# Latent stage of a two-layer decoder trunk: the query norm's root, its factors and the value projections in another order

## The chip, the cores and the metric

One core of a Trainium2 chip runs the whole trunk in one launch. The metric is the device time of a run in microseconds (us); the median over the runs of a kernel is compared. TensorE does the matmuls, VectorE (DVE) and ScalarE (ACT) the element-wise work, GpSimd (POOL) a few small operations, SyncE (SP) issues the loads.

## The reference, cut to what matters

Two layers over 256 tokens of width 1024. Each layer is: half a SwiGLU feed-forward, a mixer beside an attention to 256 memory tokens, half a SwiGLU feed-forward. Layer 0 mixes with a short convolution; layer 1 with causal latent attention (MLA), 6 heads, whose keys and values come from one shared latent made after layer 0. The change lies in layer 1's mixer:

```
c_q, q_mem = split(h @ w_in, [384])
q = (rms_norm(c_q, g_q_lora) @ w_uq).reshape(b, s, 6, 192)
q_nope = rms_norm(q[..., :128], g_q_nope)
q_rope = apply_rope(rms_norm(q[..., 128:], g_q_rope), cos, sin)
v = (c_kv @ w_ukv).reshape(b, s, 6, 256)[..., 128:]
scores = (q_nope . k_nope + q_rope . k_rope) * 192 ** -0.5      # causal
y_mix = softmax(scores) @ v
y_mem = softmax(rms_norm(q_mem) . k_mem / 8) @ v_mem            # 4 heads of 64
x = x + concat(y_mix, y_mem) @ w_out
```

## The kernel before, in words

Everything is float32. Each weight unit (up to 128 x 1024) is loaded by SP into one of 6 raw buffers (L78) and split into a rounded high part (an ACT cast, L69) and the rest (a DVE subtraction, L70) in one of 8 split buffers. A product is then three matmuls (L203 to L205: high x high, high x low, low x high), in the feed-forward two (L209, L210). The class Stream keeps the units in one list in the order in which they are used: `get` takes the next one, `pump` issues loads up to 9 units and splits up to 5 units ahead of what has been taken. A pump inside `issue_after(ins)` holds those of its instructions that lie on the engine of `ins` behind `ins`.

The code is written in the Tile framework. The order in which the code emits operations is their priority; the framework orders each engine's instructions itself, and an operation that it holds to be ready may go ahead of an earlier one that is not. It also makes all the waits, and accesses of different engines to one PSUM bank are kept apart in time. PSUM has 8 banks: two called pg (`bank()`), two called pm (`mbank()`), four accumulators (`abank(q)`).

The function `mla` does layer 1's mixer:
- It projects the normalized input to the latent query (three blocks of 128) and the memory query (two blocks). The norm of the latent query isn't applied to it: the projections run on the raw latent, and its factor F (L1018) enters the later norms through F and its square F2 (L1020).
- For each half t of the tokens it projects the rotary part of the query (`uq`), multiplies by the gain (L998), sums squares (L1003, L1004) and rotates: half 0 on DVE, half 1 on POOL (`apply_rope`, L814 to L820, six operations; both use the same temporary buffers).
- `next(mem)` runs the first part of the memory attention: column sums of the squared memory query (L615), the variance (L623, L177), the root as a power on POOL (L162, tile rsy_mq), the factor mq_rs (L632). The generator `mem_attention` gives control back at each `yield`.
- The latent query's sum of squares (L1011), variance, root on POOL (L162, tile rsy_cq), F and F2.
- Three pairs of heads are projected (the query projections, L203 to L205 with out acc or pg); each pair is copied by DVE (L1048), then squared by ACT (L1050).
- Column sums of the squares (L1058, 24 matmuls with one column each) give the heads' variances (L1063 to L1066), a root in DVE steps (L165 to L172) and the factors ra and rs (L1070 to L1074).
- Scores without the rotary part for heads 0 to 3 (L1028, in the four accumulators); the memory attention's first scores, maxima and exponentials (L641 to L658).
- `next(kv_steps)` twice: the value projections, the last steps of the generator `shared_kv` (its function `project` with s = 1; 4 times 6 matmuls of 384 columns on the latent in tiles mem_V and mem_kT), each copied out of its bank by ACT (L939).
- The rotated queries are scaled by ra (L1082) and transposed (L1086, L1087), and a pump is held behind the scaling. Scores of heads 4 and 5, rotary scores (L1093), and then softmax, transposes and value products head by head (`soft` L1100 to L1115, `value` L1121 to L1129), mixed with the steps of the memory attention (L667 to L678) by a written list, and with the output projection, which begins as soon as an accumulator is free.

Of the kernel before, what the change touches and what calls it, by code (L numbers as in the profile page):

```python
# [16 lines left out]
P = 128  # L17
# [91 lines left out]
def trunk(ctx: ExitStack, tc: tile.TileContext, a, out):  # L109
# [498 lines left out]

    def mem_attention(l, q, sq, F, outs, pe_tile):

        cs = mbank()
        for b in range(2):
            for t in range(2):
                o = 4 * t + 2 * b
                nc.tensor.matmul(cs[:, 0, o:o + 2], sq[:, b, t * P:(t + 1) * P], half2, start=(b == 0 and t == 0),  # L615
                                 stop=(b == 1 and t == 1), skip_group_check=True)
        csv = cs[:, 0, 0:8].rearrange("p (t h) -> p t h", t=2)
        if F is not None:
            fb = F.rearrange("p (t o) -> p t o", o=1).broadcast_to([P, 2, 4])
            f2 = sm.tile([P, 2], F32, name="mq_f2")  # L620
            nc.vector.tensor_tensor(out=f2, in0=F, in1=F, op=ALU.mult)
            v0 = sm.tile([P, 2, 4], F32, name="mq_v0")
            nc.vector.tensor_tensor(out=v0, in0=csv, in1=f2.rearrange("p (t o) -> p t o", o=1).broadcast_to([P, 2, 4]),  # L623
                                    op=ALU.mult)
            csv = v0
        v = mean_eps(csv, 64, [P, 2, 4], "mq")
        y = rsqrt(v, [P, 2, 4], "mq")
        rs = sm.tile([P, 2, 4], F32, name="mq_rs")
        if F is None:
            nc.vector.tensor_scalar(out=rs, in0=y, scalar1=0.125, scalar2=None, op0=ALU.mult)  # L630
        else:
            nc.vector.scalar_tensor_tensor(out=rs, in0=y, scalar=0.125, in1=fb, op0=ALU.mult, op1=ALU.mult)  # L632
        kT, mv = mem_st[l]
        yield
        for b in range(2):
            pes = []
            scs = [mbank(), mbank()]
            for t in range(2):
                for hh in range(2):
                    rows = slice(64 * hh, 64 * hh + 64)  # L640
                    nc.tensor.matmul(scs[hh][:, t, :], q[rows, b, t * P:(t + 1) * P], kT[rows, b, :], start=(t == 0),  # L641
                                     stop=(t == 1), skip_group_check=True)
            for hh in range(2):
                h = 2 * b + hh
                sc = scs[hh]
                mx = sm.tile([P, 2], F32, name="m_mx")
                nc.vector.tensor_reduce(out=mx, in_=sc, axis=AX.X, op=ALU.max)
                nb = sm.tile([P, 2], F32, name="m_nb")
                nc.vector.scalar_tensor_tensor(out=nb, in0=mx, scalar=-1.0, in1=rs[:, :, h], op0=ALU.mult, op1=ALU.mult)
                pe = pe_tile()  # L650
                se = sm.tile([P, 2], F32, name="m_se")
                for t in range(2):
                    nc.scalar.activation(out=pe[:, t, :], in_=sc[:, t, :], func=AF.Exp, bias=nb[:, t:t + 1],
                                         scale=rs[:, t, h:h + 1], accum_out=se[:, t:t + 1])
                rc = sm.tile([P, 2], F32, name="m_rc")
                nc.vector.reciprocal(out=rc, in_=se)
                for t in range(2):
                    nc.vector.tensor_scalar(out=pe[:, t, :], in0=pe[:, t, :], scalar1=rc[:, t:t + 1], scalar2=None,  # L658
                                            op0=ALU.mult)
                pes.append(pe)  # L660
            yield
            pts = []
            for hh in range(2):
                tp = mbank()
                for mt in range(2):
                    for t in range(2):
                        nc.tensor.transpose(tp[:, mt, t * P:(t + 1) * P], pes[hh][:, t, mt * P:(mt + 1) * P], ident)  # L667
                pt = wk.tile([P, 2, T], F32, name="sq")
                nc.scalar.copy(out=pt, in_=tp)
                pts.append(pt)  # L670
            yield
            g = keep(6 + b)
            ob = mbank()
            for mt in range(2):
                for hh in range(2):
                    h = 2 * b + hh
                    rows = slice(64 * hh, 64 * hh + 64)
                    nc.tensor.matmul(ob[rows, 0, :], mv[:, mt, 64 * h:64 * h + 64], pts[hh][:, mt, :], start=(mt == 0),  # L678
                                     stop=(mt == 1), skip_group_check=True)
            split(ob[:, 0, :], None, g[:, 0, :], g[:, 1, :])  # L680
            outs[6 + b] = g
            if b == 0:
                yield
            else:
                nc.scalar.activation(out=warm, in_=pe[:, 0, 0:1], func=AF.Silu, scale=0.0)
# [138 lines left out]
    def shared_kv():  # L824
# [70 lines left out]
        yield  # L895

        def project(s, c, t, w):
            b = (bank() if s else mbank()).rearrange("p a t -> p (a t)")[:, 0:384]
            for kt in range(2):
                mm3(b, (ct[kt][:, 0, t * P:(t + 1) * P], ct[kt][:, 1, t * P:(t + 1) * P]),  # L900
                    (w[:, 0, kt * 384:(kt + 1) * 384], w[:, 1, kt * 384:(kt + 1) * 384]), kt == 0, kt == 1)
            return b
# [44 lines left out]
    def mla(next_norm, pl, kv_steps):  # L947
# [43 lines left out]
        for t in range(2):  # L991
            b = abank(t).rearrange("p a t -> p (a t)")[:, 0:384]
            for k in range(3):
                ww, o = (wu0, k * 384) if k < 2 else (wu1, 0)
                mm3(b, (cq[k][:, 0, t * P:(t + 1) * P], cq[k][:, 1, t * P:(t + 1) * P]),
                    (ww[:, 0, o:o + 384], ww[:, 1, o:o + 384]), k == 0, k == 2)
            q1 = big1[:, 768 + 384 * t:1152 + 384 * t].rearrange("p (h d) -> p h d", d=64)
            nc.vector.tensor_tensor(out=q1, in0=b.rearrange("p (h d) -> p h d", d=64),  # L998
                                    in1=gc[:, GC_GQR:GC_GQR + 64].rearrange("p (o d) -> p o d", o=1).broadcast_to([P, 6, 64]),
                                    op=ALU.mult)  # L1000
            sq = wk.tile([P, 2, T], F32, name="sq")
            sqv = sq.rearrange("p a t -> p (a t)")[:, 0:384]
            nc.scalar.activation(out=sqv, in_=b, func=AF.Square)  # L1003
            nc.vector.tensor_reduce(out=msr[:, t, :], in_=sqv.rearrange("p (h d) -> p h d", d=64), axis=AX.X, op=ALU.add)  # L1004
            q2 = keep(14, (P, 6, 64), F32) if t else big1[:, 1536:1920].rearrange("p (h d) -> p h d", d=64)
            apply_rope(nc.gpsimd if t else nc.vector, q1, q2, t, 6, m_tile)
            rps.append(q2)
        next(mem)
        cs = mbank()
# [4 lines left out]
        nc.vector.tensor_tensor(out=rq2, in0=rq, in1=rq, op=ALU.mult)  # L1014
        v = sm.tile([P, 2], F32, name="cq_v")
        nc.vector.tensor_tensor(out=v, in0=cs[:, 0, 0:2], in1=rq2, op=ALU.mult)
        F = sm.tile([P, 2], F32, name="cq_F")
        nc.vector.tensor_tensor(out=F, in0=rsqrt(mean_eps(v, 384, [P, 2], "cq"), [P, 2], "cq"), in1=rq, op=ALU.mult)  # L1018
        F2 = sm.tile([P, 2], F32, name="cq_F2")
        nc.vector.tensor_tensor(out=F2, in0=F, in1=F, op=ALU.mult)  # L1020
        krT, knT, V = kv["krT"], kv["knT"], kv["V"]
        def out_of(sc, t):
            return (sc[:, 0:P], sc[:, P:384])[t]
# [5 lines left out]
                                 stop=False, skip_group_check=True)  # L1029
            return sc  # L1030

        cs = bank()
        sqs = []
        for pr in range(3):
            b = abank(2 + pr) if pr < 2 else bank()
            for s in range(2):
                n = 2 * pr + s
                if n == 0:
                    w, o = wu1, 384
                elif n % 2 == 1:  # L1040
                    w, o = W.get(("uq", 2 + n // 2)), 0
                else:
                    o = 384
                for k in range(3):
                    oo = o + k * P
                    mm3(b[:, s, :], (w[:, 0, oo:oo + P], w[:, 1, oo:oo + P]), (cq[k][:, 0, :], cq[k][:, 1, :]),
                        s == 0 and k == 0, s == 1 and k == 2)
            nc.vector.tensor_copy(out=qn[:, 2 * pr:2 * pr + 2, :], in_=b)  # L1048
            sq = (wk.tile([P, 2, T], F32, name="sq") if pr < 2 else ev.tile([P, 2, T], F32, name="ev"))
            nc.scalar.activation(out=sq, in_=b, func=AF.Square)  # L1050
            sqs.append(sq)
            if pr == 0:
                W.pump()
        for pr, sq in enumerate(sqs):
            for s in range(2):
                for t in range(2):
# [17 lines left out]
        nc.vector.scalar_tensor_tensor(out=rs, in0=y[:, 0], scalar=192.0 ** -0.5, in1=Fb, op0=ALU.mult, op1=ALU.mult)  # L1074
        scs = [scores(h) for h in range(4)]
        next(mem)
        next(kv_steps)
        next(kv_steps, None)
        for t in range(2):
            q2 = rps[t]  # L1080
            q3 = big1[:, 768 + 384 * t:1152 + 384 * t].rearrange("p (h d) -> p h d", d=64)
# [246 lines left out]
```

## Time and profile before

| what | value |
|---|---|
| median of 3 runs | 970.01 us (969.94 to 973.65) |
| the profiled execution | 971.22 us |
| its span, first to last instruction | 969.4 us |
| mean granted TensorE clock | 0.996 |
| TensorE busy | 958.2 us, 99% of the span |
| VectorE busy | 718.0 us, 74% |
| ScalarE busy | 558.7 us, 58% |
| GpSimd busy | 40.3 us, 4% |

All other times come from one execution that the hardware profiler recorded; they count from the start of its span. A busy TensorE is not TensorE at its peak: matmuls are pipelined, and their ends are modelled. The granted clock is the share of full speed (2.4 GHz) that TensorE had; the lower of its two levels is 1.2 GHz. The latent stage lies between about 704 and 785 us, where the last feed-forward begins.

### The profile page before, as it was taken

Reading aid. Unit: us, or ns where it says so; the run is one execution under the profiler, and the core shown is the slowest. Engines: PE = TensorE matmul, PEld = TensorE weight load, DVE = VectorE, ACT = ScalarE, POOL = GpSimd, SP = SyncE. Lnnn points to the kernel's source line nnn. Section 1 sums busy time; section 2 is a strip of 40 time slices with the busy share of each in tenths; the row PEclk is TensorE's granted clock in tenths of the full one; section 3 lists DMA queues with packets and bytes.
Section 4 is the critical chain, followed back from the end, with each engine's and each line's share of the span. In section 5 each row is a group of like instructions: output and inputs, shape, how many; then the busy total and the mean of one; then the engine's idle time right before and its main releaser. Section 6 shows DMA issues by size and latency. Waiting matters only on the chain.

```text
span 969.4 us, 15411 instructions
## 1 busy us (share of the span) xinstructions
PE 958.2 (99%) x5856; PEld 848.8 (88%) x5856; DVE 718.0 (74%) x1225; ACT 558.7 (58%) x963; POOL 40.3 (4%) x62
## 2 busy tenths in 40 slices
PE   9999999999999999999999999999999999999998
PEld 7889898889898888888888888888997988888887
DVE  7988767774978787777839877778558679777771
ACT  8766555554556465555645666556455666555550
POOL 1300000000000000000000300000020000000000
PEclk9999999999999999999999999999998999999999
DMA  8786556552744485555526755654523318666530
GB/s 310 238 278 204 197 192 190 180 195 67 256 157 130 142 272 196 195 174 196 194 64 205 255 196 175 200 191 161 175 96 130 111 53 290 204 195 196 179 128 17
DMA packets 50187, 174.10 MB, mean 180 GB/s; under 512 B 5696, under 2 KB 7232, under 8 KB 50112
## 3 DMA queue, kind: packets, MB, share of 16 engines
q1 hardware_dynamic: 49680, 172.45, 53.9%
q8 instruction: 46, 0.75, 0.3%
q10 hardware_dynamic: 432, 0.66, 0.2%
q14 instruction: 29, 0.24, 0.1%
HBM read 172.04 MB, written 1.05 MB: 179 GB/s over the span
## 4 chain that ended last, share of the span: by engine, by line
PE 88%; DVE 7%; DMA 2%; POOL 1%; ACT 1%; issue 1%; SPq 0%; DVEq 0%
PE pg L209 20%; PE pm L209 19%; PE pg L210 10%; PE pm L210 10%; PE acc L209 9%; PE acc L210 4%; DVE whl L70 3%; PE pg L203 2%; PE pg L204 2%; PE pg L205 2%; PE pm L203 2%; PE pm L205 2%; PE pm L204 2%; DMA wraw<-in_w 1%; PE acc L203 1%; PE acc L204 1%
## 5 line engine op out<-in xcount | busy, mean ns | idle before, releaser
L70 DVE TENSOR_TENSOR whl<-wraw,whl 128x1024 fp32r<-128x1024 f32 (+3 forms) x330 | 390.2, 1198 | 92.6 <-ACT whl L69 92.4
L69 ACT CAST whl<-wraw 128x1024 fp32r<-128x1024 f32 (+3 forms) x330 | 337.5, 1029 | 163.4 <-PE pm L210 80.6
L209 PE MATMUL pg<-xs,whl 128*128 128x512 f32 x704 | 255.7, 397 | 1.0 <-DVE ev L492 0.9
L209 PE MATMUL pm<-xs,whl 128*128 128x512 f32 x704 | 254.9, 396 | 0.5 <-DVE ev L492 0.5
L210 PE MATMUL pg<-xs,whl 128*128 128x256 f32 x704 | 196.8, 280 | 0.2 <-DVE whl L70 0.2
L210 PE MATMUL pm<-xs,whl 128*128 128x256 f32 x704 | 196.1, 279 | 0.0
L209 PEld LDWEIGHTS pm<-xs,whl 128*128 128x128 f32 x704 | 132.2, 188 | 31.5 <-DVE ev L492 0.8
L209 PEld LDWEIGHTS pg<-xs,whl 128*128 128x128 f32 x704 | 132.2, 188 | 31.4 <-DVE ev L492 1.0
L209 PE MATMUL acc<-g,whl 128*128 128x512 f32 x384 | 138.7, 397 | 0.9 <-DVE g L196 0.9
L210 PEld LDWEIGHTS pg<-xs,whl 128*128 128x128 f32 x704 | 132.6, 188 | 2.1 <-DVE whl L70 1.8
L210 PEld LDWEIGHTS pm<-xs,whl 128*128 128x128 f32 x704 | 132.5, 188 | 0.3
L210 PE MATMUL acc<-g,whl 128*128 128x256 f32 x384 | 107.0, 279 | 0.0
L209 PEld LDWEIGHTS acc<-g,whl 128*128 128x128 f32 x384 | 72.0, 188 | 19.0 <-DVE g L196 2.4
L210 PEld LDWEIGHTS acc<-g,whl 128*128 128x128 f32 x384 | 72.3, 188 | 0.0
L491 ACT COPY sq<-pm 128x256 f32<-128x256 f32 x88 | 32.8, 372 | 68.5 <-PE pm L210 68.5
L209 PE MATMUL pg<-g,whl 128*128 128x512 f32 x192 | 68.3, 398 | 0.0
L195 ACT CAST g<-gg 128x256 fp32r<-128x256 f32 x94 | 38.0, 405 | 49.7 <-DVE gg L508 45.3
L496 DVE TENSOR_TENSOR ev<-ev,R 128x512 f32<-128x512 f32 x88 | 61.1, 698 | 2.3
L209 PE MATMUL pm<-g,whl 128*128 128x512 f32 x170 | 60.4, 398 | 0.0
L492 DVE TENSOR_TENSOR ev<-pm,sq 128x256 f32<-128x256 f32 x88 | 37.2, 423 | 27.5 <-ACT sq L491 27.3
L203 PE MATMUL pg<-xs,whl 128*128 128x256 f32 x192 | 55.3, 288 | 0.0
L505 ACT ACTIVATE silu<-ev 128x256 f32<-128x256 f32 x88 | 36.5, 415 | 31.5 <-DVE ev L496 28.8
(323 smaller groups left out, 1352.5 us busy)
## 6 DMA issues: line engine op xcount, KB each, us to landing
wraw<-in_w SPq DMA_DIRECT2D x260, 512.0 KB, 4.1
wraw<-in_cin SPq DMA_DIRECT2D x20, 512.0 KB, 4.1
wraw<-in_wo SPq DMA_DIRECT2D x16, 512.0 KB, 4.3
wraw<-in_wmem SPq DMA_DIRECT2D x8, 512.0 KB, 4.3
wraw<-in_qin SPq DMA_DIRECT2D x5, 512.0 KB, 4.5
wraw<-in_mem SPq DMA_DIRECT2D x4, 512.0 KB, 3.8
wraw<-in_wukv SPq DMA_DIRECT2D x4, 384.0 KB, 3.3
wraw<-in_uq SPq DMA_DIRECT2D x4, 384.0 KB, 3.5
```

Source lines behind the costliest of these rows:

```text
L69: nc.scalar.copy(out=h[:, 0, o:o + n], in_=r[:, o:o + n])
L70: nc.vector.tensor_tensor(out=h[:, 1, o:o + n], in0=r[:, o:o + n], in1=h[:, 0, o:o + n].bitcast(F32), op=ALU.subtract)
L195: first = nc.scalar.copy(out=hi, in_=src)
L203: nc.tensor.matmul(o, lhs[0], rhs[0], start=start, stop=False, skip_group_check=True)
L204: nc.tensor.matmul(o, lhs[0], rhs[1], start=False, stop=False, skip_group_check=True)
L205: nc.tensor.matmul(o, lhs[1], rhs[0], start=False, stop=stop, skip_group_check=True)
L209: nc.tensor.matmul(o, lhs[0], x, start=start, stop=False, skip_group_check=True)
L210: nc.tensor.matmul(o[:, 0, :], lhs[1], x[:, 0, :], start=False, stop=stop, skip_group_check=True)
L491: nc.scalar.copy(out=part[:, s, :], in_=ps[s][:, 1, :])
L492: nc.vector.tensor_tensor(out=e[:, s, :], in0=ps[s][:, 0, :], in1=part[:, s, :], op=ALU.add)
L496: evac = nc.vector.tensor_tensor(out=e, in0=e, in1=rb(st["R"]), op=ALU.mult)
L505: act = nc.scalar.activation(out=sl, in_=e[:, 0, :], func=AF.Silu)
```

## The change

Four edits, all in the functions printed above. In `mem_attention`, control goes back right behind the root, so that mq_rs is emitted with the memory scores. In `shared_kv`, the value projections of the second token half take a pm bank instead of a pg bank. In `mla`, the rotation of half 1 on POOL is emitted behind the latent query's root, and F and F2 are made later. The two steps of the value projections, and the bank of the column sums, are emitted right behind the query projections.

```
@@ mem_attention
         y = rsqrt(v, [P, 2, 4], "mq")
+        yield
         rs = sm.tile([P, 2, 4], F32, name="mq_rs")
...
         kT, mv = mem_st[l]
-        yield
@@ shared_kv
         def project(s, c, t, w):
-            b = (bank() if s else mbank()).rearrange("p a t -> p (a t)")[:, 0:384]
+            b = (bank() if s and not t else mbank()).rearrange("p a t -> p (a t)")[:, 0:384]
@@ mla
-            apply_rope(nc.gpsimd if t else nc.vector, q1, q2, t, 6, m_tile)
+            if t == 0:
+                apply_rope(nc.vector, q1, q2, t, 6, m_tile)
             rps.append(q2)
         next(mem)
...
-        F = sm.tile([P, 2], F32, name="cq_F")
-        nc.vector.tensor_tensor(out=F, in0=rsqrt(mean_eps(v, 384, [P, 2], "cq"), [P, 2], "cq"), in1=rq, op=ALU.mult)
-        F2 = sm.tile([P, 2], F32, name="cq_F2")
-        nc.vector.tensor_tensor(out=F2, in0=F, in1=F, op=ALU.mult)
+        y_cq = rsqrt(mean_eps(v, 384, [P, 2], "cq"), [P, 2], "cq")
+        apply_rope(nc.gpsimd, q1, rps[1], 1, 6, m_tile)
...
-        cs = bank()
         sqs = []
         for pr in range(3):
...
+        next(kv_steps)
+        next(kv_steps, None)
+        cs = bank()
+        F = sm.tile([P, 2], F32, name="cq_F")
+        nc.vector.tensor_tensor(out=F, in0=y_cq, in1=rq, op=ALU.mult)
+        F2 = sm.tile([P, 2], F32, name="cq_F2")
+        nc.vector.tensor_tensor(out=F2, in0=F, in1=F, op=ALU.mult)
         for pr, sq in enumerate(sqs):
...
         scs = [scores(h) for h in range(4)]
         next(mem)
-        next(kv_steps)
-        next(kv_steps, None)
         for t in range(2):
```

## Rows read from the trace of the kernel before

**Rows 1.** The page: busy time, share of the span and instructions of each engine.

```profile
PE 958.2 (99%) x5856; PEld 848.8 (88%) x5856; DVE 718.0 (74%) x1225; ACT 558.7 (58%) x963; POOL 40.3 (4%) x62
```

**Rows 2.** Stretches: us, busy of PE, PEld, DVE, ACT, POOL, PE clock, DMA share, GB/s.

```profile
721.00:726.00 5.00, 3.03 (x26) 2.89 (x25) 1.77 (x6) 2.40 (x4) 1.43 (x3) 1.00 0.00 0
726.00:733.20 7.20, 7.20 (x30) 5.44 (x28) 3.22 (x13) 0.57 (x2) 0.00 (x0) 0.53 0.25 75
733.20:749.00 15.80, 14.17 (x89) 11.21 (x89) 15.22 (x42) 11.41 (x32) 0.00 (x0) 1.00 0.49 166
749.00:785.00 36.00, 36.00 (x278) 33.91 (x274) 26.06 (x66) 27.63 (x68) 0.00 (x0) 1.00 0.28 89
```

**Rows 3.** The chain that ended last, 716 to 724: start, us, what.

```profile
716.65 0.59 POOL g L814
...
717.79 1.59 POOL rsy_mq L162
...
721.85 0.68 POOL rsy_cq L162
...
722.90 0.60 DVE xs L1048
...
723.60 0.61 ACT sq L1050
```

**Rows 4.** Timeline of PE, 721 to 749: start, us, what [idle before <- releaser].

```profile
721.33 0.95 PE L1058 MATMUL pg<-ones,sq 128*128 128x1 f32 x8
724.25 1.05 PE L1058 MATMUL pg<-ones,sq 128*128 128x1 f32 x8 [1.97 <-ACT sq L1050]
725.16 3.01 PE L1028 MATMUL acc<-spare,xs 128*128 128x128 f32 x12
...
733.43 0.34 PE L204 MATMUL pg<-whl,mem_V 128*128 128x384 f32 x1
...
736.23 0.34 PE L205 MATMUL pg<-whl,mem_kT 128*128 128x384 f32 x1
737.62 0.44 PE L203 MATMUL pg<-whl,mem_V 128*128 128x384 f32 x1 [1.05 <-ACT spare L939]
...
739.90 0.92 PE L1028 MATMUL pg<-spare,xs 128*128 128x128 f32 x4
740.66 0.71 PE L667 MATMUL pm<-ident,g 128*128 128x128 f32 x5
...
748.01 0.61 PE L1121 MATMUL pm<-ident,g 128*128 128x128 f32 x3 [0.58 <-DVE g L1115]
```

**Rows 5.** Timeline of DVE, 709 to 744.

```profile
709.34 0.96 DVE L70 TENSOR_TENSOR whl<-wraw,whl 128x768 fp32r<-128x768 f32 x1 [0.24 <-ACT whl L69]
...
726.10 1.23 DVE L70 TENSOR_TENSOR whl<-wraw,whl 128x1024 fp32r<-128x1024 f32 x1 [1.72 <-ACT whl L69]
729.70 0.17 DVE L1063 TENSOR_TENSOR vv<-pg,cq_F 128x12 f32<-128x12 f32 x1 [2.37 <-PE pg L1058]
...
731.85 0.18 DVE L170 SCALAR_TENSOR_TENSOR rst_qh<-rsy_qh 128x24 f32<-128x24 f32 x1
733.19 0.69 DVE L647 TENSOR_REDUCE m_mx<-pm 128x2 f32<-128x512 f32 x1 [1.16 <-PE pm L641]
...
735.13 0.56 DVE L1082 TENSOR_TENSOR xs<-xs,q_ra 128x384 f32<-128x384 f32 x1
...
739.52 3.49 DVE L70 TENSOR_TENSOR whl<-wraw,whl 128x1024 fp32r<-128x1024 f32 x3
743.30 1.02 DVE L1100 TENSOR_TENSOR ev<-acc,mask 128x384 f32<-128x384 f32 x2 [0.29 <-PE acc L1093]
```

**Rows 6.** Timeline of ACT, 724 to 738.

```profile
724.09 1.98 ACT L69 CAST whl<-wraw 128x1024 fp32r<-128x1024 f32 x2
...
737.07 0.88 ACT L939 COPY spare<-pg 128x384 f32<-128x384 f32 x2
```

**Rows 7.** The chain that ended last, layer 0's memory scores, at full clock.

```profile
271.67 1.06 PE pm L641 x8
```

## The prediction

> **What bounds the kernel now.** I read the busy totals first: TensorE is busy for 99% of the span [rows 1], so a change that removes no matmul can win only time in which TensorE stands still or runs slowly. Then the table of stretches, to see where that is. In the latent stage, 721 to 726 holds only 3.03 us of matmul time out of 5.00; 726 to 733.2 is all busy, but at a granted clock of 0.53, close to the lower of its two levels (1.2 of 2.4 GHz); from 733.2 on the clock is back at 1.00; and from 749 to 785 no time is lost [rows 2]. Third, the chain of waits says why: POOL begins the rotation, makes the memory query's root, goes on with the rotation, and only at 721.85 begins the latent query's root. DVE waits for that with the factor cq_F and has the second copy of the query projections (L1048) queued behind it; ACT's square (L1050) needs that copy [rows 3], and TensorE's column sums (L1058) need the square. Last, TensorE's own timeline prices the stage: 1.97 us idle ahead of the second group of column sums, 1.05 us ahead of the last value projection, 0.58 us ahead of the first transposes of the softmax [rows 4]. With the slow stretch, 7.2 us x (1 - 0.53) = 3.4 us, that is 1.97 + 1.05 + 0.58 + 3.4 = **7.0 us lost between 721 and 749**. This is all that the change can win here.
>
> **The change, part by part.** The order of each engine's instructions is made by the framework from what it estimates to be ready, earliest in the code first; the trace departs from the code's order (the memory root stands inside the rotation [rows 3]). So I work with the dependences and treat the order as uncertain.
>
> *The root ahead of the rotation, the factors later.* No operation is added or removed: six rotation products, two roots and two factor products exist before and after. The memory factor mq_rs, for which DVE waited ahead of the latent query's variance, is now emitted with the memory scores. If POOL takes the roots one behind the other, the second ends at about 717.79 + 1.59 + 0.68 = 720.1; if the rotation still goes first, it ends at 722.5 as before [rows 3]. Nothing needs cq_F until the column sums are done (728.3, below), and the rotated queries not until after that, so either order costs TensorE nothing. The cover is the value projection; without it a late root would cost the old 1.97 us again.
>
> *Value projections right behind the query projections.* They are 24 matmuls in both kernels. Sixteen steps, from 733.43 to 736.23, take 2.80 us, 0.175 each [rows 4]; 24 take 4.2 us. The query projections end where the first column sum starts, at 721.33 [rows 4], so they run from 721.3 to 725.5. Their weights are there: the last 768-column split began at 709.34 [rows 5]. No load and no split is issued at the moved place: both projections take their units from the stream without the call that issues more, and the next such call finds the same count before and after, so nothing is moved past anything in the load queue.
>
> *Alternating banks.* Before, all four projections took the two pg banks, and the last stood 1.05 us for ACT's copies out of them [rows 4], made only from 737.07 on [rows 6]. Now every second one takes a pm bank. The third still needs the bank of the last query projections, so the copy and the square of those must end by 723.5. ACT has, from about 720.1, one square of 0.61, two casts of 1.98 together, the second square of 0.61 [rows 3, 6]: to 723.3. That fits with little to spare; I take 0, and as the upper bound 1.4 us (the second square behind a late cq_F, at 724.9 instead of 723.5). The four copies, 0.44 each [rows 6], end by 725.5, before anyone needs their banks.
>
> *What is late next.* From 724.25 to 725.16 eight column sums take 0.91 us [rows 4], so 24 take 2.7 us and end at 728.3. DVE's chain of variance, root and scaling starts there instead of at 729.70. From 729.70 to 731.85 ten steps take 2.15 us, 0.215 each; then DVE stood 1.16 us for the memory scores, slowed by the low clock, and did two maxima inside the chain. The scaled queries (L1082) came 5.4 us after the start [rows 5]. Sixteen steps without that take 3.4 us: 731.7 instead of 735.13, **3.4 us earlier**. Meanwhile TensorE has the sixteen latent scores, 3.0 us (four take 0.76, from 739.90 to 740.66 [rows 4]), and the memory scores, 1.06 [rows 7]: to 732.4, so no gap there.
>
> But the value projections were the filler from 733 to 738.8, and they are used up. From 732.4 TensorE has only 46 small matmuls (transposes, eight scores, rotated and memory products; by the spacings above, 0.11 to 0.19 each, an estimate of 5 to 9 us) until the first softmax weights are ready. That is set by DVE. Between the scaled queries and the first masked scores (L1100, 743.30) DVE does five weight splits that are held behind the scaling (the last three take 3.49 us) and the memory softmax [rows 5]. In the new order the two maxima (0.6 each) fall behind the scaling too. So L1100 comes 3.4 - 1.2 = 2.2 us earlier, or 3.4 if one of the five splits goes into DVE's idle time ahead of 728. The 4.7 us from L1100 to the first softmax transposes (748.01) stay. From 749 on TensorE was dense [rows 2], so the shift goes through to the end one to one; the 0.58 us gap and a few products of the output projection may fill as well. **Sum: a gain of 2.2 to about 5 us; I take 3.5**, the later split's bound and a trace of filling, since DVE had idle time for that split before (1.72 and 2.37 us ahead of 726.10 and 729.70 [rows 5]). Put otherwise, 7.0 us lost becomes 3.5 us idle, all of it between 732 and 745.
>
> The profiled execution took 971.22 us, 1.8 more than its span; less 3.5 it is 967.7. It lies 1.2 above the median of the runs (970.01), so against those I write 966.5.
>
> **Clock.** The clock fell at about 726, after the gap of 1.97 us and column sums of one column on both sides of it, and stayed up after 1.05 us and 0.58 us [rows 2, 4]. The transposes at 740.66 ran in a stretch granted 1.00 [rows 2, 4]. The Trainium skill, page "TensorE: Matmul & The Clock Gate", section "Part 4: PE-mode transpose", says that a transpose does not count as TensorE activity the way another matmul does. By that rule the thinned stretch from 732 to 745, with its transposes, would look idle and the clock would fall in it; the sum would then be rival 2's, some 971 to 973. The rows do not decide it, since their transposes stood next to dense work.
>
> **Rivals.**
> 1. *DVE gives back more.* A split that becomes ready early (the value weights free two buffers sooner) is put inside the root chain, 1.16 us, or the third projection stands 1.4 us. For it: DVE's chain was filled in that way at 733.19 [rows 5]. Against: those 4 us of idle time that DVE has ahead of the chain. Gain 0 to 2.2: 967.8 to 970.0. Chance 0.20.
> 2. *The cover is gone and the clock falls again (slower).* Between the memory scores and the scaled queries or the memory transposes TensorE stands in one piece for more than the 1.05 us that left the clock up, towards the 1.97 that did not; this decides it. A slow stretch like the last one reaches into the dense output projection: 3.4 us back, on a gain of 2.2, so 971.2, and up to 1.5 more where slowed products feed DVE late: 972.7. For: about 3.5 us of idle time must lie somewhere in 732 to 745. Against: it is in pieces, among matmuls of 128 and 256 columns. Chance 0.10.
> 3. *POOL's order does not change in effect* (rotation still first) and DVE's factor still stands ahead of the third copy. The gap is covered by the projections except for the 1.4 us at the third: a gain of 2.1, 967.9. Chance 0.07.
> 4. *TensorE can fill nearly everything*: output products go ahead of the softmax, so 5 to 7 us are won: 963.0 to 965.0. Against: the accumulators hold scores until DVE has masked them. Chance 0.13.
>
> **How the numbers follow.** The forecast, a gain of 2.2 to 5 (965.0 to 967.8), has 0.50. About 0.5% (4.85 us) is what a measurement of this kernel can tell from no change. Faster by more than that needs rival 4 or the forecast's uppermost part: 0.13 + 0.03 = 0.16. Slower by more (above 974.9) lies beyond all cases worked out: 0.03 for what I have not seen. Same: 0.81. The range takes the forecast, rivals 1 and 3 and half of rival 4, with 0.4 for scatter at the upper end: 964.0 to 970.4; it leaves out rival 2 and the rest of 4, about 0.17.
>
> **What would show it.** In the new profile: value projections directly behind the query projections with no gap over 0.5 us up to the last column sum; granted clock 1.00 from 726 to 733; the variance chain starting 1.2 to 1.5 us earlier and the scaled queries about 3.4 us earlier; then some 3.5 us of TensorE idle time, ended by DVE and ACT, ahead of the first softmax transposes; from there both kernels alike, shifted. I am wrong if a stretch at half clock remains in the stage, if L1100 is not at least 2 us earlier, or if the shift is lost again before the last feed-forward.

## The result and the profile after

The changed kernel takes **978.04 us** (median of 4 runs, 977.13 to 978.6) against 970.88 us of the kernel before in the same session (4 runs, 969.94 to 973.65): ratio 1.0066 [1.0044, 1.0089], so slower by 0.66%. The prediction (966.5 us, 964.0 to 970.4) had the wrong sign, and the time lies outside its range.

The busy totals, which answer to [rows 1]: the same 5856 matmul instructions cost 4.1 us more.

```profile
PE 962.3 (99%) x5856; PEld 852.4 (87%) x5856; DVE 718.6 (74%) x1225; ACT 558.9 (57%) x963; POOL 40.3 (4%) x62
```

The latent stage, from its first L301 to the L301 of the last feed-forward, as one stretch in each kernel (before, then after): us, busy of PE, PEld, DVE, ACT, POOL, PE clock, DMA share, GB/s.

```profile
704.36:785.00 80.64, 77.03 (x547) 70.09 (x546) 57.70 (x154) 51.67 (x118) 7.09 (x10) 0.96 0.32 103
```

```profile
703.14:791.47 88.33, 81.65 (x547) 73.75 (x546) 58.64 (x154) 52.14 (x118) 7.06 (x10) 0.92 0.29 95
```

The stage is 88.33 - 80.64 = 7.7 us longer. TensorE's idle time in it grew from 80.64 - 77.03 = 3.6 to 88.33 - 81.65 = 6.7 us, and the same 547 recorded matmuls took 4.6 us more, at a mean clock of 0.92 instead of 0.96. The span grew by only 975.8 - 969.4 = 6.4 us, since the changed kernel reaches the stage 704.36 - 703.14 = 1.2 us earlier. A gap of 0.91 us on TensorE in layer 0 is gone in it (e12 below); the rest can't be told from scatter, for in the kernels below the stage starts anywhere from 702.15 to 704.43, with that gap or without.

Where the time lies, stretch by stretch in the changed kernel (same columns; answers to [rows 2]):

```profile
720.10:725.30 5.20, 2.25 (x14) 1.93 (x12) 2.66 (x7) 3.01 (x5) 1.07 (x2) 1.00 0.00 0
725.30:728.40 3.10, 3.09 (x13) 3.09 (x13) 1.94 (x2) 2.04 (x4) 0.00 (x0) 0.69 0.34 107
728.40:736.60 8.20, 8.20 (x36) 7.84 (x36) 2.67 (x13) 1.52 (x2) 0.00 (x0) 0.50 0.28 89
736.60:743.00 6.40, 3.38 (x21) 2.10 (x20) 5.16 (x14) 2.60 (x10) 0.00 (x0) 0.99 0.25 82
743.00:746.60 3.60, 3.49 (x14) 2.70 (x14) 3.60 (x8) 0.44 (x2) 0.00 (x0) 0.57 0.79 244
```

Two holes, 720 to 725 and 737 to 743, and behind each a stretch at the lower clock: 3.10 x 0.31 + 8.20 x 0.50 = 5.1 us and 3.60 x 0.43 = 1.5 us lost there, against 3.4 us in the kernel before. TensorE's timeline (answers to [rows 4]) names the waits:

```profile
722.01 0.34 PE L205 MATMUL pm<-whl,mem_kT 128*128 128x384 f32 x1
725.31 0.44 PE L203 MATMUL pg<-whl,mem_V 128*128 128x384 f32 x1 [2.96 <-ACT ev L1048]
...
728.40 3.41 PE L1063 MATMUL pg<-ones,sq 128*128 128x1 f32 x16
731.67 1.84 PE L1063 MATMUL pg<-ones,ev 128*128 128x1 f32 x8
...
740.83 1.15 PE L1089 MATMUL pg<-ident,xs 128*128 128x128 f32 x6 [1.91 <-DVE xs L1085]
743.11 2.58 PE L1027 MATMUL pg<-spare,xs 128*128 128x128 f32 x8 [1.14 <-ACT xs L1090]
...
754.62 0.61 PE L1124 MATMUL pm<-ident,g 128*128 128x128 f32 x3 [0.51 <-DVE g L1118]
```

The value projections were to fill the old gap; the third of the four now stands for 2.96 us itself, because the square of the last query projections (`ev`, L1048) frees its bank late. The chain of waits says why (start, us that the chain spends there, what; answers to [rows 3]):

```profile
716.57 1.59 POOL rsy_mq L162
...
719.96 0.66 POOL rsy_cq L162
...
720.64 0.56 DVE cq_F L1056
...
721.59 0.07 DVE xs L1046
...
722.29 0.04 ACT sq L1048
...
722.78 1.98 ACT whl L69 x2
724.76 0.51 ACT ev L1048
```

DVE's timeline (answers to [rows 5]) shows the factor still ahead of the second and the third copy, and later the root chain:

```profile
720.64 0.55 DVE L1056 TENSOR_TENSOR cq_F<-rsy_cq,rsy_x 128x2 f32<-128x2 f32 x1 [1.89 <-POOL rsy_cq L162]
...
721.51 0.68 DVE L1046 COPY xs<-acc 128x512 f32<-128x512 f32 x1
...
722.18 0.68 DVE L1046 COPY xs<-pg 128x512 f32<-128x512 f32 x1
...
733.55 0.17 DVE L1068 TENSOR_TENSOR vv<-pg,cq_F 128x12 f32<-128x12 f32 x1 [5.33 <-PE pg L1063]
...
736.01 1.22 DVE L70 TENSOR_TENSOR whl<-wraw,whl 128x1024 fp32r<-128x1024 f32 x1
...
738.95 1.29 DVE L647 TENSOR_REDUCE m_mx<-pm 128x2 f32<-128x512 f32 x2 [1.21 <-PE pm L641]
...
740.22 0.55 DVE L1085 TENSOR_TENSOR xs<-xs,q_ra 128x384 f32<-128x384 f32 x1
...
747.64 0.56 DVE L1103 TENSOR_TENSOR ev<-acc,mask 128x384 f32<-128x384 f32 x1 [0.61 <-PE acc L1096]
...
751.41 0.42 DVE L196 TENSOR_TENSOR g<-pm,g 128x256 fp32r<-128x256 f32 x1 [1.81 <-ACT g L195]
751.76 0.15 DVE L1110 SCALAR_TENSOR_TENSOR a_nb<-a_mx,q_rs 128x2 f32<-128x2 f32 x1
```

The code emits the factor behind all three copies, yet DVE waited 1.89 us for it with two copies queued behind it. From 754.62 on both kernels are alike: 754.62 to 791.47 is 36.85 us, and 748.01 [rows 4] to 785.00 was 36.99.

### The profile page after: what moved, and what is told of

It reads as the page before. It is cut to its first block, busy times and chain, and to the rows that moved or that the text cites. A ratio compares the mean times of both kernels' runs of the same rounds, so it can differ in the third digit from the quotient of the medians.

```text
span 975.8 us, 15414 instructions
## 1 busy us (share of the span) xinstructions
PE 962.3 (99%) x5856; PEld 852.4 (87%) x5856; DVE 718.6 (74%) x1225; ACT 558.9 (57%) x963; POOL 40.3 (4%) x62
## 3 DMA queue, kind: packets, MB, share of 16 engines
HBM read 172.04 MB, written 1.05 MB: 177 GB/s over the span
## 4 chain that ended last, share of the span: by engine, by line
PE 91%; DVE 5%; DMA 1%; ACT 1%; POOL 1%; issue 1%; SPq 0%; DVEq 0%; ACTq 0%
PE pg L209 20%; PE pm L209 20%; PE pg L210 10%; PE pm L210 10%; PE acc L209 9%; PE acc L210 4%; PE pg L203 3%; PE pg L205 2%; PE pg L204 2%; DVE whl L70 2%; PE pm L203 2%; PE pm L205 2%; PE pm L204 2%; PE acc L203 1%; PE acc L204 1%; PE acc L205 1%
```

## The experiments

Theory A: the late factor ahead of the copies on DVE makes the third projection stand, and the clock falls behind that. Theory B: in the new place the projections are missing later, as cover for the root chain. A rival cause, GpSimd's new order, would need neither. "Stage" is the length between the two L301 as above, "idle" what of it TensorE was not busy, both in the profiled execution; the intervals are 95%. The kernel before was run again beside each group of kernels: its median was 971.49 us beside e1 to e4, 971.38 beside e5 to e8 and 970.95 beside e9 to e12. Differences of medians between groups are good to about that scatter.

| kernel | median us | ratio to before | stage | idle | clock in stage |
|---|---|---|---|---|---|
| changed kernel | 978.04 | 1.0066 [1.0044, 1.0089] | 88.33 | 6.68 | 0.92 |
| e1 before + yield | 969.35 | 0.999 [0.9967, 1.0013] | 79.29 | 3.91 | 0.98 |
| e2 changed, factors held | 971.66 | 1.0014 [0.9992, 1.0036] | 80.92 | 4.14 | 0.98 |
| e3 before + projections and banks | 976.38 | 1.0078 [1.0051, 1.0105] | 86.67 | 6.79 | 0.94 |
| e4 before + yield, rotation, held factors | 965.1 | 0.9939 [0.992, 0.9959] | 75.56 | 2.03 | 1.00 |
| e5 changed, filler matmuls | 971.92 | 1.0004 [0.9993, 1.0016] | 82.18 | 3.87 | 1.00 |
| e6 e4, half the projections early | 966.73 | 0.995 [0.9932, 0.9967] | 76.55 | 2.73 | 1.00 |
| e7 e4 + alternating banks, projections ahead of memory | 967.36 | 0.9965 [0.9951, 0.9979] | 78.00 | 2.06 | 1.00 |
| e8 e2, maxima later | 971.1 | 0.9993 [0.9978, 1.0007] | 82.25 | 4.62 | 0.98 |
| e9 e4 without the rotation edit | 965.75 | 0.994 [0.9918, 0.9962] | 75.56 | 2.03 | 1.00 |
| e11 e4 + alternating banks | **963.84** | **0.9922 [0.9898, 0.9946]** | 74.50 | 1.00 | 1.00 |
| e12 e4 without the yield | 965.93 | 0.9941 [0.9917, 0.9964] | 75.62 | 2.04 | 1.00 |

**Which part does the harm.** e1 makes only the first edit of the change (the yield), e3 only the value projections and the alternating banks; e2 keeps the whole change and holds the factors on DVE:

```
+            copied = nc.vector.tensor_copy(out=qn[:, 2 * pr:2 * pr + 2, :], in_=b)
...
+        with tc.issue_after(copied.ins):
+            nc.vector.tensor_tensor(out=F, in0=y_cq, in1=rq, op=ALU.mult)
+            nc.vector.tensor_tensor(out=F2, in0=F, in1=F, op=ALU.mult)
```

> The kernel before with one edit alone: the memory attention gives control back right behind its root, so that mq_rs is made later, in layer 0 (the convolution mixer) and in layer 1. Theory A (the loss of the change comes from the third value projection, which stands for its bank because the factor cq_F is ahead of the query copies on VectorE): this edit has no part in the loss; it removes the 0.91 us TensorE gap in layer 0 and the 1.5 us wait for the root there, so 1.0 to 1.5 us faster than before, and in layer 1 POOL makes the latent root up to 0.7 us earlier, so another 0 to 1 us: 1.0 to 2.5 us faster in all. Theory B (the value projections are missed later as filler): the same. If it is not faster, the 1.2 us by which the changed kernel is ahead when the latent stage begins have another source.

> The changed kernel, with the factor and its square held on VectorE behind the third copy of the query projections, so that neither copy waits for POOL. Theory A: the 2.96 us gap ahead of the third value projection goes (below 0.5 us), the clock stays at 1.00 there, and 6 to 8 us come back: 970 to 972, level with before or a little faster. Theory B: the first gap may go too, but the time is lost again between the memory scores and the softmax, where the projections are missing: 975 or more, with TensorE gaps of more than 4 us together there.

> The kernel before with the value projections moved right behind the query projections and on alternating banks, and nothing else: rotation, root, factors and the memory factor as before. Theory A: the same gap ahead of the third projection, some 0.7 us longer because the factor comes later (3.3 to 4 us), the same fall of the clock, and layer 0's 1.2 us not won: 979 to 981. Theory B: the same or a little less. A rival C, by which the POOL order causes the loss, expects about the time of before, 969 to 972.

e1 is 971.49 - 969.35 = 2.1 us under the kernel before, as expected, but its interval holds 1, so the yield's worth isn't shown by the time; it does no harm. e3 came out below the 979 to 981 written down; still it alone is about as slow as the whole change, with the same three gaps on TensorE:

```profile
725.45 0.69 PE L203 MATMUL pg<-whl,mem_V 128*128 128x384 f32 x1 [3.07 <-ACT ev L1049]
739.21 1.15 PE L1086 MATMUL pg<-ident,xs 128*128 128x128 f32 x6 [1.91 <-DVE xs L1082]
741.50 2.20 PE L1028 MATMUL pg<-spare,xs 128*128 128x128 f32 x8 [1.14 <-ACT xs L1087]
```

In e3 the latent root is still behind the whole rotation (GpSimd starts it at 720.63, behind L820), so GpSimd's order isn't the cause. In e2 the third projection follows at once and the column sums run at full clock (first the stretch of the sums, then the score transposes' gaps):

```profile
725.66:732.20 6.54, 6.53 (x49) 5.59 (x48) 4.10 (x15) 1.52 (x2) 0.00 (x0) 1.00 0.45 152
```

```profile
734.40 1.15 PE L1090 MATMUL pg<-ident,xs 128*128 128x128 f32 x6 [2.22 <-DVE xs L1086]
736.69 2.40 PE L1027 MATMUL pg<-spare,xs 128*128 128x128 f32 x8 [1.14 <-ACT xs L1091]
```

That is theory A: two instructions of DVE held back give 978.04 - 971.66 = 6.4 us (as expected, 970 to 972). But e2 is no faster than the kernel before, though it has no gap at the sums any more: a gap of 2.22 us has opened later, where the projections used to run, and in the profiled execution the clock fell behind that one and the next (1.14 us), to 0.50 from 738 to 740:

```profile
738.00:739.00 1.00, 1.00 (x5) 0.71 (x4) 1.00 (x2) 0.00 (x0) 0.00 (x0) 0.50 0.98 401
```

**The same hold with the projections at their old place.** e4 is e2 without the last two edits of the change (projections and banks back).

> The kernel before with the POOL edits (memory factor later, rotation emitted behind the root) and the two factors held on VectorE behind the third copy; the value projections stay where they were, behind the memory scores. Theory A: no copy waits for POOL, so the 1.97 us gap and the stretch at half clock go, the projections are still there as filler, and layer 0 gives 1.2: 6 to 8 us faster than before, 963 to 965. Theory B: the same. Rival C: about as before. If the 1.97 us gap is gone and the clock falls all the same, the gap was not what lowered it.

```profile
732.13 0.44 PE L203 MATMUL pg<-whl,mem_V 128*128 128x384 f32 x1 [1.41 <-ACT spare L939]
742.50 0.55 PE L1125 MATMUL pm<-ident,g 128*128 128x128 f32 x3 [0.62 <-ACT g L653]
```

These are all its gaps over 0.5 us from 716 to 758. e4 beats both kernels, and against e2 the last two edits together cost 971.66 - 965.1 = 6.6 us. e11 below differs from e2 by the projections' place alone, and there the place costs 971.66 - 963.84 = 7.8 us: theory B. Holding the factors cures the gap that the change set out from: e9 and e12 below share only the hold among the edits, and the gap is gone in both. The moved projections are a loss with the hold (e2) and without it (e3).

**Is it the idle time that lowers the clock?** e5 puts twelve matmuls without use into the gap of the changed kernel (the profile lists each of them as two instructions):

```
         next(kv_steps)
+        dm = mbank()
+        for _ in range(12):
+            nc.tensor.matmul(dm[:, 0, 0:P], ones, ones, start=True, stop=True, skip_group_check=True)
         next(kv_steps, None)
```

> The changed kernel with twelve matmuls on a tile of ones (128 columns each, result unused) put on TensorE between the second and the third projection, where it stood idle for 2.96 us. The factor is still late, so the third projection starts at the same time as in the changed kernel. If the idle stretch is what lowers the granted clock afterwards, the gap ahead of the third projection is all but gone, the clock stays at 1.00 from there to the end of the column sums (it was 0.50 for about 9 us), and some 4 to 5 us come back: 972 to 974. If the clock falls for what follows (single column sums and transposes) whatever was ahead, nothing comes back: 977 to 979.

```profile
723.30 2.84 PE L1055 MATMUL pm<-ones 128*128 128x128 f32 x24
726.45 0.44 PE L203 MATMUL pg<-whl,mem_V 128*128 128x384 f32 x1 [0.31 <-ACT ev L1048]
...
736.58 0.55 PE L1092 MATMUL pg<-ident,xs 128*128 128x128 f32 x3 [1.41 <-DVE xs L1088]
```

```profile
726.40:735.20 8.80, 8.72 (x60) 7.78 (x60) 5.19 (x15) 3.60 (x6) 0.00 (x0) 1.00 0.42 121
```

The third projection is as late as before (5.2 us behind the first), but the clock stays at 1.00, and 978.04 - 971.92 = **6.1 us** come back, a little more than the 4 to 5 expected. All ten executions had a mean clock of 0.998 or more, the four of the changed kernel 0.991 to 0.993. So in this place it is TensorE's standing that brings the clock down, and what TensorE does slowly afterwards costs more than the wait of 2.96 us itself. The late projection and the missing cover are still in e5: it is 971.92 - 965.1 = 6.8 us slower than e4.

**How much cover, and which.** e6 is e4 with the first two projections (one weight unit, both token halves) early and on alternating banks, the other two late; e7 is e4 with all four directly ahead of the second `next(mem)` and on alternating banks; e8 is e2 with the second `next(mem)` behind the scaling loop.

> The run with both roots' products ahead of the rotation and the factors held behind the third copy (965.1), with the first two value projections right behind the query projections and the other two at the old place. If the projections at the old place are cover that the latent stage's root chain needs in full, half of them leaves a gap ahead of the score transposes of about 2 us and perhaps a clock fall: 968 to 971. If half is cover enough, the time is that of the run it starts from: 964 to 966. Below 964 only if the earlier projections fill idle time of TensorE, of which that run has none at the column sums.

> As the run with 965.1, but all four value projections directly behind the memory scores instead of behind the memory sums, and with the alternating banks. The idle 1.41 us in front of the memory's sums, which waits on a copy of the value projections on ScalarE, should go or move. If TensorE's order alone decides, 963 to 965; if the memory's exponentials are then late because copies stand ahead of them on ScalarE, the chain behind the memory's sums is later by some 1 to 3 us: 966 to 968.

> The changed kernel with the factors held behind the third copy (971.66), and with the memory's maxima put behind the scaled queries on VectorE. If the maxima, which ran ahead of the scaled queries, make the 2.22 us gap ahead of the score transposes, that gap falls to about 1 us and the time to 970 to 971. If the gap is made by the root's own chain with no cover left on TensorE, it stays near 2 us and the time at 971 to 973.

e6 (966.73) and e7 (967.36) came out between the cases that were written down and in the worse one, and every run of both is slower than e4's slowest (965.67). e7 differs from e11 below by the place alone, 967.36 - 963.84 = 3.5 us; the memory's first exponential starts 29.7 us after the stage in it and 25.5 in e4, as the worse case had it, but what of the 3.5 us that makes isn't shown. In e8 the gap went from 2.22 to 1.24 us as expected, and the time is 971.1: within the scatter of e2, so the maxima ahead of the scaled queries are at most a small part of theory B.

```profile
733.15 1.07 PE L1089 MATMUL pg<-ident,xs 128*128 128x128 f32 x6 [1.24 <-DVE xs L1085]
```

**What the other edits are worth.** e9 is e4 with the rotation at its old place in the code, e12 is e4 without the yield, e11 adds the edit of the banks to e4.

> The kernel before with the yield behind the root and the factors held on VectorE behind the third copy; the rotation on GpSimd stays ahead of the latent root and the value projections stay at their old place. If only the factor's place on VectorE matters (the prediction's step that either order of GpSimd costs TensorE nothing), the time is that of the run with the rotation moved as well, 964 to 966. If the root's end, 1.9 us later in this order, reaches the variance chain behind the column sums, it is 966 to 968.

> The run with 965.1, with the alternating banks added. The value projections stay at their old place, so the second one must now wait for a pm bank that the memory's scores hold until their exponentials have run, and the third no longer for two ScalarE copies. If the 1.41 us gap ahead of the third projection was worth its length, 963.5 to 964.5; if the wait for the exponentials takes its place, 965 to 967.

> The run with 965.1 without the moved yield, so that the memory factor is emitted directly behind its root again, in both layers. In layer 0 a gap of 0.91 us on TensorE should come back, 0.6 to 0.9 us. In layer 1 VectorE waits again for the memory root ahead of the latent variance; if that delays the latent root past the third copy, the column sums may again be late and the time 967 to 970; if it doesn't, 965.5 to 966.5.

e9 doesn't test what its expectation says: GpSimd's order in it is that of e4 (root at 721.24, ahead of L820), so it is the yield that brought the root ahead of one rotation product, and the rotation edit changed nothing. The test is e12, where the root starts at 722.05, behind L820: its stage is 75.62 us against 75.56, so GpSimd's order is worth nothing that shows once the factors are held. The latent root on GpSimd in e9 and in e12, then what comes back in layer 0 of e12, which uses the same generator:

```profile
721.24 0.69 POOL L162 TENSOR_TENSOR rsy_cq<-var_cq,mhalf 128x2 f32<-128x2 f32 x1
722.05 0.71 POOL L162 TENSOR_TENSOR rsy_cq<-var_cq,mhalf 128x2 f32<-128x2 f32 x1
```

```profile
250.66 0.50 PE L209 MATMUL acc<-g,whl 128*128 128x512 f32 x1 [0.90 <-DVE g L196]
```

The kernel before has this gap too (0.91 us, at 250.81); with the yield it is gone. By the time alone (965.93 against 965.1) that isn't resolved. e11 is the fastest: the 1.41 us gap ahead of the third projection became one of 0.81 us ahead of the transposes, and the stage is 1.06 us shorter. Its interval overlaps that of e4, so that last microsecond rests on the stage of one execution each.

```profile
729.35 0.52 PE L1090 MATMUL pg<-ident,xs 128*128 128x128 f32 x3 [0.81 <-DVE xs L1086]
```

## Why the prediction was wrong, step by step

In the prediction's own terms: 7.0 us lost were to become 3.5 of idle time. They became 2.96 + 1.91 + 1.14 + 0.51 = 6.5 us of idle time and 5.1 + 1.5 = 6.6 us at the lower clock. Less the old 7.0 that is 6.1 of the stage's 7.7 us; the rest isn't put down to a cause.

- **What bounds the kernel**: right. The 7.0 us between 721 and 749 were there to be won in the execution that was profiled; e11's stage is 80.64 - 74.50 = 6.1 us shorter.
- **Root ahead of the rotation, "either order costs TensorE nothing"**: this is the step that failed first. For GpSimd it holds (e12). But "nothing needs cq_F until the column sums are done" looked only at who reads it, and not at who stands behind it on DVE: two copies, the last square, and the bank of the third projection.
- **Alternating banks, "I take 0 ... upper bound 1.4 us"**: the measured wait is 2.96 us (3.07 in e3). The sum to 723.3 has ACT's order right (a square, two casts, the last square; it took 722.29 to 725.27, 2.98 us against 3.2), but it starts at the end of the root, as if the second copy did not wait behind the factor. The upper bound does let the square wait, and it comes to 724.9 only without the two casts of 1.98 us between the two squares. In the kernel before they stood there too, with the factor as late as in that bound, and the last square ended at 725.97 + 0.60 = 726.6 (row behind this list), 3.1 us after the 723.5 that the prediction allows: the trace of before had the price. The late factor was there as a bound and as rival 3, which had the mechanism at less than half its price and without a clock fall.
- **Clock**: the text wanted 1.00 from 726 to 733, on the ground that 1.97 us had lowered it and 1.05 had not; by that same ground a wait of 2.96 us would have had a fall in its price. About 5.1 us went there, and e5, where the clock stays up, gives 6.1 us for both falls together. The rule of the Trainium skill (page "TensorE: Matmul & The Clock Gate", section "Part 4: PE-mode transpose"), by which a transpose doesn't count as activity the way another matmul does, is neither shown nor refuted here: the clock fell behind transposes and gaps at 741 to 743 in the changed kernel and at 734 to 737 in e2, but e6 ran transposes with 0.49 us of busy time in a stretch of 2.90 us, and there it stayed at 1.00 (row below).
- **What is late next, "sixteen steps ... 3.4 us"**: mis-sized. From the first variance to the scaled queries it was 740.22 - 733.55 = 6.7 us, and 733.79 - 728.43 = 5.4 in e2, since the framework put a split (1.22 us) and both maxima into the chain, which in the changed kernel also waited 1.21 us for the memory scores; in e4, with the maxima alone, 4.2. That is rival 1's mechanism, and with the used-up cover it makes rival 2's: gaps of 1.91 and 1.14 us and a second clock fall. The mechanisms of rivals 1, 2 and 3 all came true together; I had priced them as alternatives.
- **"The 4.7 us from L1100 to the first softmax transposes stay"**: wrong, 754.62 - 747.64 = 7.0. The memory product (L196) stands ahead of the first softmax's bias on DVE, and waits 1.81 us for memory results that are now later (rows above). In e4 it is 742.50 - 737.75 = 4.75.
- **"From 749 on TensorE was dense, so the shift goes through one to one"**: right, with the sign reversed: the first softmax transposes came 754.62 - 748.01 = 6.6 us later, the end of the stage 791.47 - 785.00 = 6.5.
- **Layer 0** was overlooked: the yield takes a gap of 0.9 us on TensorE out of it.

ACT's last square in the kernel before:

```profile
725.97 0.60 ACT L1050 ACTIVATE ev<-pg 128x512 f32<-128x512 f32 x1
```

## What to carry to other kernels

On an engine that works through its queue in order, as DVE did here, an operation that nobody needs soon still delays whatever is queued behind it; when a scheduler may put it there, emitting it later in the code is no guarantee, and an explicit hold behind the urgent instruction did it here (e2, e4). Before moving filler work into a gap, ask what the gap's cause is (here two instructions of 128 x 2 elements) and what the filler covers where it stands. And walk every queue instruction by instruction up to the one that frees the resource: the price of a late input is that input plus all that stands between on the last engine.

## What was not expected of the hardware

**The same order of work gets different clocks.** e8 and e2 have the same instructions on TensorE up to the memory scores. In e2's profiled execution the column sums and latent scores ran at 1.00 (row above), and so did the column sums in e8's; there the clock fell to 0.62 over the latent scores, with no idle time over 0.5 us since the projections:

```profile
726.31:730.77 4.46, 4.46 (x19) 3.65 (x18) 3.77 (x17) 0.43 (x1) 0.00 (x0) 0.62 0.23 89
```

And a gap of 2.41 us inside this stretch of e6 left it at 1.00, there and from 734.5 to 740:

```profile
731.60:734.50 2.90, 0.49 (x4) 0.25 (x3) 2.90 (x7) 2.72 (x10) 0.00 (x0) 1.00 0.01 4
```

```profile
734.50 0.55 PE L1090 MATMUL pg<-ident,xs 128*128 128x128 f32 x3 [2.41 <-ACT spare L939]
```

So in this kernel a fall can't be read off the length of one gap, which is how I had argued. e2 and e8 ran on different chips, but the clock also differs between executions of one kernel on one chip: the kernel before, beside e1 to e4, had mean clocks from 0.993 to 1.000. Over all groups it took 966.3 to 967.4 us in the executions at 1.000, and 972.9 to 973.9 in those at 0.993, whereas e4, whose clock was never under 0.999, stayed within 964.05 to 965.67. So the 3.4 us that the prediction read off one profile as lost to the clock are not lost in every execution. By these groups the larger part of what e4 gains over the median of the kernel before is that its clock doesn't fall: against the four executions of before at 1.000 it gains only 1 to 2 us. Not all scatter is the clock's: e7, at 0.998 to 1.000, took 966.32 to 970.09. What decides in which execution the clock falls stays open.
